# Attention score products in two passes of 128 rows, and where the value and modulation tiles lie

## The chip, the core and the metric

The kernel runs on one NeuronCore of a Trainium2 chip. The metric is device time in microseconds (us) from launch to end, the median of several runs; lower is better. The profile is that of one execution. Its engines are PE (TensorE, matrix products), PEld (the loading of weights into it), DVE (VectorE), ACT (ScalarE), POOL (GpSimd) and SP, whose queue issues most of the loads from memory.

## The reference

Two layers of a diffusion transformer block on 256 latent tokens and 256 context tokens, of width 1024. In each layer one projection feeds four mixers side by side: a Fourier mixer, differential attention, grouped-query attention and a convolution. They are merged by gates, projected once and followed by an MLP with a squared ReLU. The part that matters here is the score products:

```python
def _diff_attention(dq, dk, dv, lam):
    s = jnp.einsum('bqhjd,bkhjd->bhjqk', dq, dk).astype(jnp.float32) * ATTN_SCALE
    p = jax.nn.softmax(s, axis=-1)
    a = (p[:, :, 0] - lam * p[:, :, 1]).astype(dv.dtype)
    return jnp.einsum('bhqk,bkhe->bqhe', a, dv)

def _gqa_attention(gq, gk, gv):
    s = jnp.einsum('bqhgd,bkhd->bhgqk', gq, gk).astype(jnp.float32) * ATTN_SCALE
    p = jax.nn.softmax(s, axis=-1).astype(gv.dtype)
    return jnp.einsum('bhgqk,bkhd->bqhgd', p, gv)
```

The head dimension d is 64. There are 4 differential heads with two score products (j) each, and 8 grouped query heads on 2 key heads. Layer 0 has latent queries on 512 keys and context queries on 256 keys; layer 1 has only the latent queries.

## The kernel before

Everything is fp32, and each product is made of fp32r parts: a number is split into a high part (rounded by ACT, L126 or L129) and a low part (what is left, subtracted by DVE, L127 or L130). An ordinary product (`mm3`, L147) has three passes: high x high (L149), low x high (L150), high x low (L151). Weights come by SP's queue into 3 landing tiles, and are split by ACT and DVE into tiles `wh` and `wl` (`chunk`, L135).

A score product has a contraction of 64, half of the 128 rows. So the kernel stacks the parts: in a stacked tile one half of the rows holds the high part and the other half the low part (`split_stack`, L496). For differential attention `split_twice` (L501) makes three tiles for each q: two with the high part of product j in both halves (L504 and the ACT copy L505), and one with the low parts of both products. `softmax_part` (L531) then runs two passes through `mms` (L154, the matmul is L156): 128 rows, q high against the stacked k, and 64 rows, q low against k high (`diff_front`, L554). For grouped attention (`gqa_front`, L604) the first pass is the stacked q against k high in both halves, and the second has 64 rows, q high against k low.

A planner orders the instructions of each engine ahead of time, by priority and by its own costs, and sets the waits; each engine then runs its own list in order. `attention_part` (L899) makes per layer the convolution projection, the Fourier mixer, the value tiles `dv`, then 4 heads of differential attention (units of 128 queries, the next head's projections and the gates of finished branches filled in between by `fill`), then 4 pairs of grouped heads in the same manner. Taps of the convolution are put on DVE unit by unit.

Tiles of 128x512 are taken from and given back to a pool `rs` (`Slots`, L55; 24 in layer 0, 16 and 14 narrow ones in layer 1). In layer 0 another 4 lie in a region that is lent until differential attention ends (`lent`, L927): the first two of the four pairs of `dv` take these (`rs.lend`), the other two pairs take tiles of `rs`. When the region is given up (L1012), the conditioning rows `srow` are loaded into it (`mods_rows`, L266). They are multiplied on DVE (L287, `mods_dve`) with rows of the modulation weights, which POOL's queue loads (L283) into two landing tiles `wm` (L922) that lie outside the lent region.

Of the kernel before, what the change touches and what calls it, by code (L numbers as in the profile page):

```python
# [9 lines left out]
F = mybir.dt.float32  # L10
R = mybir.dt.float32r
# [8 lines left out]
P = 128  # L20
D = 1024
KT = 8
L = 256
T = 512
# [56 lines left out]
class Body:  # L81
# [20 lines left out]
    def new(self, name, shape, dtype=F, pool=None, space=None):  # L102
        if space is not None:
            pool = getattr(self, "psum", None)
            if pool is None:
                pool = self.psum = self.ec(self.tc.tile_pool(name="psum", bufs=1, space=PSUM))
        return (pool or self.const).tile(shape, dtype, tag=name, name=name)
# [393 lines left out]
    def split_twice(self, dst, src, scale=None):  # L501
        for j in range(2):
            a, b = slice(64 * j, 64 * j + 64), slice(64 - 64 * j, 128 - 64 * j)
            self.split_to(dst[j][a], dst[2][a], src[a], scale)  # L504
            self.nc.scalar.activation(dst[j][b], src[a], AF.Copy, scale=scale or 1.0)  # L505

    def rope_split(self, dst, ps, n, split, gain=None):
        nc = self.nc
        if n > L:
            split([d[:, L:n] for d in dst], ps[:, L:n], gain)  # L510
        raw, sw, t1 = (self.tmp()[:, :L] for _ in range(3))
        if gain is None:
            nc.scalar.copy(raw, ps[:, :L])
        else:
            nc.scalar.activation(raw, ps[:, :L], AF.Copy, scale=gain)  # L515
        nc.vector.stream_shuffle(sw, raw, list(range(16, 32)) + list(range(16)))
        nc.vector.tensor_tensor(t1, raw, self.cos, op=ALU.mult)
        nc.vector.tensor_tensor(sw, sw, self.sin, op=ALU.mult)
        nc.vector.tensor_tensor(t1, t1, sw, op=ALU.add)
        split([d[:, :L] for d in dst], t1)  # L520
# [33 lines left out]
    def diff_front(self, l, s, qt, dq, dk):  # L554
        nc = self.nc
        k0, nk, t0 = self.keys[s]
        er = []
        for j in range(2):
            pr = slice(64 * j, 64 * j + 64)
            q = [x[:, s * L:(s + 1) * L] for x in (dq[j], dq[2][pr])]  # L560
            k = [x[:, k0:k0 + nk] for x in (dk[j], dk[j][pr])]
            er.append(self.softmax_part(q, k, nk, qt))
        (e0, z0), (e1, z1) = er
        r1, c1 = self.sm1(), self.sm1()
        nc.vector.reciprocal(r1, z1)
        nc.vector.scalar_tensor_tensor(c1, z0, self.nlam[:, l:l + 1], r1, ALU.mult, ALU.mult)
        nc.vector.scalar_tensor_tensor(e0, e1, c1, e0, ALU.mult, ALU.add)
        if qt == 0:
            self.zz = self.st4()[:, :2]
        nc.vector.scalar_tensor_tensor(self.zz[:, qt:qt + 1], z0, EPS, z0, ALU.mult, ALU.mult)  # L570
        return e0, self.zz
# [31 lines left out]

    def gqa_front(self, l, j, s, i, qt, gq, gk):  # L604
        k0, nk, t0 = self.keys[s]
        qr = slice(64 * i, 64 * i + 64)
        c = 4 * self.ns * j + 2 * (2 * s + qt) + i
        q = [x[:, s * L:(s + 1) * L] for x in (gq[i], gq[i][qr])]
        k = [x[:, k0:k0 + nk] for x in (gk[j // 2][0], gk[j // 2][1][qr])]
        e, z = self.softmax_part(q, k, nk, qt, self.st32[1][:, c:c + 1])  # L610
        r = self.sm1()
        self.mark = self.nc.vector.reciprocal(r, z).ins.name
        if l or (2 * s + qt) in GACT:
            self.nc.scalar.activation(e, e, AF.Copy, scale=r)
        else:
            self.nc.vector.tensor_scalar(e, e, r, None, ALU.mult)
        return e
# [281 lines left out]
    def attention_part(self, l, n):  # L899
# [11 lines left out]
        with ExitStack() as ctx:  # L911
            pool = ctx.enter_context(tc.tile_pool(name=f"mix{l}", bufs=1, reuse_waits="tile"))
# [5 lines left out]
            spare = new("or", [P, 2 * L])  # L918
            self.oraw = Ring([spare[:, j * L:(j + 1) * L] for j in range(2)])
            self.more_weights(new, 0 if l == 0 else 2)  # L920
            if l == 0:
                wm = self.ring("wmg", NWG, [P, D], pool=pool)  # L922
            lent = ExitStack()
            tiles = [new(f"r{i}", [P, T], R) for i in range(wide)] + [new(f"q{i}", [P, L], R) for i in range(thin)]
            pts = Ring([[new(f"pt{q}{i}", [P, 4, L], R) for q in range(2)] for i in range(2)])
            self.pt = pts
            spool = lent.enter_context(tc.tile_pool(name=f"lent{l}", bufs=1, reuse_waits="tile"))  # L927
            rs = self.rs = Slots(tiles, [self.new(f"e{i}", [P, T], R, spool) for i in range(4 if l == 0 else 0)])
            self.tmps["g"] = self.gring if l == 0 else Ring([g[:, i * L:(i + 1) * L] for g in self.gring.tiles for i in range(2)])

            for k in ((0, 5) if "dbg" in self.a else ()):
# [11 lines left out]
            dv = []  # L943
# [13 lines left out]
            def head(i):  # L957
                def k():
                    dk = self.pair()
                    self.rope_split(dk, self.proj(l, T_DK + i, T), T, self.split_stack)  # L960
                    heads[i] = [dk]

                def q():
                    dq = self.few(n, 3)
                    self.rope_split(dq, self.proj(l, T_DQ + i, n), n, self.split_twice, gain=SCALE)
                    heads[i].append(dq)
                return [k, q]

            gq, box = [], {}
# [38 lines left out]
            self.advance(backs, -1)  # L1008
            if PIPE[0]:
                self.advance(backs)  # L1010
            rs.give(dv[2:] if l == 0 else dv)
            lent.close()  # L1012
            if l == 0:
                spool = ctx.enter_context(tc.tile_pool(name="rows", bufs=1, reuse_waits="tile"))
                self.mods_rows(wm, self.new("srow", [P, 2, D], pool=spool), spare.bitcast(BF))
            gk = box["gk"]
            while backs and not LATE:
# [256 lines left out]
MU, NWG = (6, 1, 0), 2  # L1274
# [117 lines left out]
```

## Time and profile before

| | |
|---|---|
| median of 3 runs | 1547.14 us |
| lowest and highest run | 1542.46 and 1548.66 us |
| span of the profiled execution, first to last instruction | 1540.8 us |
| PE busy | 1486.1 us (96%) |
| DVE busy | 1196.6 us (78%) |
| ACT busy | 793.7 us (52%) |

The profile has no separate time for the profiled execution; its span is set against the median. Matmuls are pipelined: the duration that the profile shows of one is longer than the time from its start to the start of the next, so what PE needs for one is read from the starts. Rows written by one line and one shape family are merged in a timeline (x2 is two instructions), with the shape of the first.

### The profile page before, as it was taken

The page shows a single profiled execution, that of the slowest core. Times are in us where ns is not written, and L with a number is a line of the kernel's source. Part 1 is how long each engine was busy: PE and PEld are TensorE (multiplying, and loading weights), DVE is VectorE, ACT ScalarE, POOL GpSimd, SP SyncE. Part 2 cuts the span into 40 slices and gives each one's busy share as a digit, 9 for nine tenths or more (in the row PEclk, how much of TensorE's full clock was granted, in tenths as well). Part 3 has the DMA queues.
Part 4 walks back from the last instruction along what each step waited for, and adds up shares of the span by engine and source line. Part 5 has one row for each costly group of instructions (what it writes and reads, how often), then busy time and mean ns, then how long its engine had stood idle before and what let it go on. Part 6 is the DMA issues. An engine that isn't in the chain of part 4 may idle for free.

```text
span 1540.8 us, 24989 instructions
## 1 busy us (share of the span) xinstructions
PE 1486.1 (96%) x9242; PEld 1305.5 (85%) x9242; DVE 1196.6 (78%) x2689; ACT 793.7 (52%) x1560; POOL 123.7 (8%) x165
## 2 busy tenths in 40 slices
PE   6999999999999999999999999989999999899997
PEld 4787778777777899898889999988798999899986
DVE  5699887888888958848975577789998976675555
ACT  4335654565554346764432336543665775577643
POOL 0100000002111002201110012100000110000000
PEclk9999999999999999999999999999999999999999
DMA  8522222313334554766775565362232435466552
GB/s 319 179 68 75 66 66 66 110 55 123 100 128 135 191 175 138 238 196 218 241 258 186 190 222 166 105 202 71 86 109 79 138 122 176 134 190 200 165 191 96
DMA packets 74009, 230.01 MB, mean 149 GB/s; under 512 B 8480, under 2 KB 17184, under 8 KB 72608
## 3 DMA queue, kind: packets, MB, share of 16 engines
q1 hardware_dynamic: 60192, 181.10, 36.1%
q0 software_dynamic: 13408, 47.19, 9.4%
q8 instruction: 72, 1.18, 0.3%
q14 instruction: 49, 0.40, 0.1%
q10 hardware_dynamic: 288, 0.14, 0.0%
HBM read 227.35 MB, written 1.05 MB: 148 GB/s over the span
## 4 chain that ended last, share of the span: by engine, by line
PE 86%; DVE 7%; DMA 3%; ACT 2%; issue 1%; SPq 0%; POOL 0%; DVEq 0%; ACTq 0%; POOLq 0%
PE ps_mm L149 22%; PE ps_mm L151 21%; PE ps_mm L150 21%; PE ps_s L156 4%; PE ps_s L438 3%; PE ps_tp L549 2%; PE ps_tp L438 1%; PE ps_o L438 1%; DVE wl L127 1%; PE ps_o L156 1%; PE ps_o L150 1%; PE ps_o L151 1%; PE ps_o L149 1%; PE ps_s L149 1%; PE ps_s L150 1%
## 5 line engine op out<-in xcount | busy, mean ns | idle before, releaser
L126 ACT CAST wh<-raw 128x1024 fp32r<-128x1024 f32 (+3 forms) x283 | 259.7, 919 | 335.1 <-PE ps_mm L150 182.8
L127 DVE TENSOR_TENSOR wl<-raw,wh 128x1024 fp32r<-128x1024 f32 (+3 forms) x283 | 303.6, 1074 | 146.6 <-ACT wh L126 142.4
L149 PE MATMUL ps_mm<-h,wh 128*128 128x512 f32 (+2 forms) x996 | 347.5, 351 | 6.2 <-ACT h L132 4.0
L151 PE MATMUL ps_mm<-h,wl 128*128 128x512 f32 (+2 forms) x996 | 345.8, 347 | 4.0 <-DVE wl L127 3.9
L150 PE MATMUL ps_mm<-h,wh 128*128 128x512 f32 (+2 forms) x996 | 343.9, 345 | 0.0
L149 PEld LDWEIGHTS ps_mm<-h,wh 128*128 128x128 f32 x996 | 190.2, 192 | 34.1 <-issue 4.6
L151 PEld LDWEIGHTS ps_mm<-h,wl 128*128 128x128 f32 x996 | 191.3, 192 | 29.1 <-DVE wl L127 6.5
L150 PEld LDWEIGHTS ps_mm<-h,wh 128*128 128x128 f32 x996 | 191.5, 192 | 21.3 <-DVE h L133 0.6
L127 DVE TENSOR_TENSOR wlx<-raw,whx 128x1024 fp32r<-128x1024 f32 (+2 forms) x85 | 94.0, 1107 | 36.9 <-ACT whx L126 36.8
L126 ACT CAST whx<-raw 128x1024 fp32r<-128x1024 f32 (+2 forms) x85 | 80.9, 953 | 47.7 <-PE ps_mm L150 29.2
L800 DVE SCALAR_TENSOR_TENSOR cy<-cv,half_dw,cy 128x512 f32<-128x512 f32 (+1 forms) x180 | 102.9, 611 | 0.2
L149 PE MATMUL ps_mm<-h,whx 128*128 128x256 f32 (+2 forms) x336 | 99.1, 296 | 3.6 <-ACT tf L515 2.5
L287 DVE SCALAR_TENSOR_TENSOR tl<-wm,srow 128x1024 bf16<-128x1024 f32 x80 | 97.6, 1220 | 0.9
L150 PE MATMUL ps_mm<-h,whx 128*128 128x256 f32 (+2 forms) x336 | 97.6, 291 | 0.0
L151 PE MATMUL ps_mm<-h,wlx 128*128 128x256 f32 (+2 forms) x336 | 97.1, 292 | 0.0
L149 PE MATMUL ps_mm<-r,wh 128*128 128x256 f32 (+1 forms) x260 | 88.1, 339 | 0.1
L151 PE MATMUL ps_mm<-r,wl 128*128 128x256 f32 (+1 forms) x260 | 86.3, 332 | 1.5 <-DVE wl L127 1.5
L150 PE MATMUL ps_mm<-r,wh 128*128 128x256 f32 (+1 forms) x260 | 86.1, 331 | 0.0
L126 ACT CAST hs<-hid 128x256 fp32r<-128x256 f32 x96 | 38.5, 406 | 70.9 <-PE ps_o L438 39.4
L149 PEld LDWEIGHTS ps_mm<-h,whx 128*128 128x128 f32 x336 | 63.5, 189 | 7.5 <-ACT tf L515 2.7
L127 DVE TENSOR_TENSOR hs<-hid,hs 128x256 fp32r<-128x256 f32 x96 | 42.4, 445 | 34.5 <-ACT hs L126 33.9
L856 POOL TENSOR_TENSOR x<-x,tg 128x512 f32<-128x512 f32 (+1 forms) x32 | 37.3, 1165 | 388.4 <-DVE tg L854 309.0
(395 smaller groups left out, 3563.7 us busy)
## 6 DMA issues: line engine op xcount, KB each, us to landing
raw<-in_wff SPq DMA_DIRECT2D x135, 512.0 KB, 4.2
raw<-in_wcol SPq DMA_DIRECT2D x88, 512.0 KB, 3.5
wm<-in_wmodT POOLq DMA_DIRECT2D x56, 512.0 KB, 4.2
wmg<-in_wmodT POOLq DMA_DIRECT2D x24, 512.0 KB, 3.8
raw<-in_wout SPq DMA_DIRECT2D x24, 512.0 KB, 4.1
boot<-in_wmod SPq DMA_DIRECT2D x8, 1024.0 KB, 8.0
raw<-in_wuc SPq DMA_DIRECT2D x16, 384.0 KB, 3.3
raw<-in_wdv SPq DMA_DIRECT2D x8, 512.0 KB, 3.5
```

The lines of the kernel that those rows point to most:

```text
L126: nc.scalar.copy(hi, src)
L127: return nc.vector.tensor_tensor(lo, src, hi.bitcast(F), op=ALU.subtract)
L149: i = nc.tensor.matmul(out, w[0], x[0], start=start, stop=False, skip_group_check=shared)
L150: nc.tensor.matmul(out, w[0], x[1], start=False, stop=False, skip_group_check=shared)
L151: nc.tensor.matmul(out, w[1], x[0], start=False, stop=stop, skip_group_check=shared)
L156: self.nc.tensor.matmul(out[:w.shape[-1]], w, x, start=start and i == 0, stop=stop and i == len(passes) - 1)
L287: i = nc.vector.scalar_tensor_tensor(self.junk, w, 1.0, self.srow[:, s, :], ALU.mult, ALU.mult, accum_out=self.mods[:, l, c, s:s + 1])
L438: self.nc.tensor.matmul(banks[t][i][:, c], x[q][:, tok], w[j][:, a:b], start=start and j + q == 0, stop=stop and q == 1, skip_group_check= ...
L549: nc.tensor.transpose(ps[:, i * P:(i + 1) * P], p[:, i * P:(i + 1) * P], self.ident)
L800: nc.vector.scalar_tensor_tensor(y3, src, w, y3, ALU.mult, ALU.add)
L856: eng.tensor_tensor(mg, mg, th, op=ALU.add)
```

## The change

In `split_twice` the low part of each q gets a tile of its own, and a new ACT instruction copies it into the other half of the rows; a q has four tiles instead of three (`few(n, 4)`). The second pass of a differential score product is the low part of q in both halves against the whole stacked k; it now includes low x low. In `gqa_front` the second pass is the whole stacked q against k low in both halves, again with low x low. So both passes contract over 128 rows.

To make room, the lent region has 8 tiles instead of 4, and holds all four pairs of `dv`; no tile of `dv` is given to `rs` in layer 0 any more. The two landing tiles `wm` are made after the lent region has been given up, in the pool that also holds `srow`.

```diff
@@ split_twice
-            self.split_to(dst[j][a], dst[2][a], src[a], scale)
+            self.split_to(dst[j][a], dst[2 + j][a], src[a], scale)
             self.nc.scalar.activation(dst[j][b], src[a], AF.Copy, scale=scale or 1.0)
+            self.nc.scalar.copy(dst[2 + j][b], dst[2 + j][a].bitcast(F))
@@ diff_front
-            pr = slice(64 * j, 64 * j + 64)
-            q = [x[:, s * L:(s + 1) * L] for x in (dq[j], dq[2][pr])]
-            k = [x[:, k0:k0 + nk] for x in (dk[j], dk[j][pr])]
+            q = [x[:, s * L:(s + 1) * L] for x in (dq[j], dq[2 + j])]
+            k = [dk[j][:, k0:k0 + nk]] * 2
@@ gqa_front
-        qr = slice(64 * i, 64 * i + 64)
-        q = [x[:, s * L:(s + 1) * L] for x in (gq[i], gq[i][qr])]
-        k = [x[:, k0:k0 + nk] for x in (gk[j // 2][0], gk[j // 2][1][qr])]
+        q = [gq[i][:, s * L:(s + 1) * L]] * 2
+        k = [x[:, k0:k0 + nk] for x in gk[j // 2]]
@@ attention_part
-            if l == 0:
-                wm = self.ring("wmg", NWG, [P, D], pool=pool)
...
-            rs = self.rs = Slots(tiles, [self.new(f"e{i}", [P, T], R, spool) for i in range(4 if l == 0 else 0)])
+            rs = self.rs = Slots(tiles, [self.new(f"e{i}", [P, T], R, spool) for i in range(8 if l == 0 else 0)])
...
-                    dq = self.few(n, 3)
+                    dq = self.few(n, 4)
...
-            rs.give(dv[2:] if l == 0 else dv)
+            rs.give([] if l == 0 else dv)
             lent.close()
             if l == 0:
                 spool = ctx.enter_context(tc.tile_pool(name="rows", bufs=1, reuse_waits="tile"))
+                wm = self.ring("wmg", NWG, [P, D], pool=spool)
                 self.mods_rows(wm, self.new("srow", [P, 2, D], pool=spool), spare.bitcast(BF))
```

## Rows read from the trace of the kernel before

**Rows 1.** The page's first part: busy us, share of span, instructions of each engine.
```profile
PE 1486.1 (96%) x9242; PEld 1305.5 (85%) x9242; DVE 1196.6 (78%) x2689; ACT 793.7 (52%) x1560; POOL 123.7 (8%) x165
```

**Rows 2.** The chain of work that ended last, by engine.
```profile
PE 86%; DVE 7%; DMA 3%; ACT 2%; issue 1%; SPq 0%; POOL 0%; DVEq 0%; ACTq 0%; POOLq 0%
```

**Rows 3.** PE's waits: who waited for whom, us in total, times, longest.
```profile
PE ps_mm L151 <- DVE wl L127: 5.5, 7, 1.5
```

**Rows 4.** Windows: stretch, its length, busy us (instructions) by engine, clock, DMA.
```profile
134.00:165.00 31.00, 30.13 (x129) 22.18 (x128) 28.96 (x69) 18.96 (x48) 0.00 (x0) 1.00 0.22 75
165.00:300.00 135.00, 134.91 (x695) 109.34 (x694) 113.47 (x358) 70.93 (x173) 0.53 (x1) 1.00 0.24 74
300.00:480.00 180.00, 178.32 (x849) 140.83 (x848) 150.30 (x354) 99.58 (x197) 27.65 (x26) 1.00 0.32 103
1060.00:1165.00 105.00, 99.54 (x625) 83.83 (x624) 97.91 (x272) 62.35 (x147) 0.00 (x0) 1.00 0.30 99
1165.00:1290.00 125.00, 123.67 (x927) 114.42 (x928) 102.58 (x276) 81.99 (x162) 13.62 (x16) 0.97 0.36 115
```

**Rows 5.** The same windows, PE instructions that write the score tile alone.
```profile
134.00:165.00 31.00, 5.94 (x16) 1.00 0.22 75
165.00:300.00 135.00, 19.48 (x50) 1.00 0.24 74
300.00:480.00 180.00, 24.04 (x62) 1.00 0.32 103
1060.00:1165.00 105.00, 13.85 (x32) 1.00 0.30 99
1165.00:1290.00 125.00, 14.53 (x32) 0.97 0.36 115
```

**Rows 6.** PE's timeline around one score product: start, duration, instruction.
```profile
155.73 0.59 PE L156 MATMUL ps_s<-r,r 128*128 128x256 f32 x2
156.25 0.50 PE L151 MATMUL ps_mm<-r,wl 128*128 128x512 f32 x1
156.59 0.40 PE L149 MATMUL ps_mm<-r,wh 128*128 128x512 f32 x1
156.82 0.40 PE L150 MATMUL ps_mm<-r,wh 128*128 128x512 f32 x1
```

**Rows 7.** The weight loads of the same stretch; in brackets the time without one.
```profile
155.94 0.18 PEld L156 LDWEIGHTS ps_s<-r,r 64*128 64x128 f32 x1 [0.25 <-issue]
156.25 0.19 PEld L151 LDWEIGHTS ps_mm<-r,wl 128*128 128x128 f32 x1
156.36 0.19 PEld L149 LDWEIGHTS ps_mm<-r,wh 128*128 128x128 f32 x1
```

**Rows 8.** Timelines of PE and PEld: value products with 64-column low halves.
```profile
347.34 1.09 PE L156 MATMUL ps_o<-pt,r 128*128 128x256 f32 x8
348.27 0.38 PE L549 MATMUL ps_tp<-consts,ta 128*128 128x128 f32 x2
...
347.92 0.30 PEld L156 LDWEIGHTS ps_o<-pt,r 128*64 128x64 f32 x2
```

**Rows 9.** ACT's copies of high parts (min/median/max ns), and waits, 134 to 300.
```profile
L505 ACT ACTIVATE r<-tf x8: 414/416/418, 144.2 to 233.2; 64x256 fp32r<-64x256 f32 x8
...
ACT r L505 <- DVE r L130: 5.2, 6, 2.3
```

**Rows 10.** PE's timeline at the first scores; in brackets its idle time and releaser.
```profile
144.68 1.36 PE L156 MATMUL ps_s<-r,r 128*128 128x512 f32 x3 [0.87 <-ACT r L505]
```

**Rows 11.** Timelines, landing tile: last value product, first use, landing times, POOL's next.
```profile
293.04 0.28 PE L151 MATMUL ps_o<-pt,r 128*128 128x256 f32 x1
...
L287 DVE SCALAR_TENSOR_TENSOR or<-wmg,srow x48: 1200/1218/2201, 353.0 to 535.6; 128x1024 bf16<-128x1024 f32 x48
DMA to landing us min/median/max: 3.5/3.8/5.8
...
329.40 1.75 POOL L856 TENSOR_TENSOR x<-x,tg 128x512 f32<-128x512 f32 x1 [48.58 <-DVE st L172]
```

## What the change does to the time, told ahead

> **What bounds the kernel now.** I read the busy shares first: TensorE (PE) is busy 1486.1 of 1540.8 us, VectorE (DVE) 1196.6, ScalarE (ACT) 793.7 [rows 1]. The chain that ended last says the same from the other side: 86% of it is PE, 7% DVE, 3% DMA [rows 2]. So PE idles only 54.7 us in all, and the largest wait outside the start-up is small: the third matmul of a weight tile for DVE's low half of that tile, 5.5 us in seven times [rows 3]. A microsecond taken from PE's own work should therefore come off the end, as long as DVE, which makes the low halves, keeps up. Whether it can is read stage by stage [rows 4]: around the score products DVE is busy 28.96 of 31 us, 113.47 of 135, 150.30 of 180, 97.91 of 105 and 102.58 of 125. Those are the five stretches in which score products run [rows 5]: 16 + 50 + 62 + 32 + 32 = 192 matmuls, two passes each, so 96 second passes, and the second pass is the one that contracts over 64 rows (8 + 25 + 31 + 16 + 16).
>
> **What a 64-row pass costs.** In the PE timeline an ordinary matmul of 512 columns starts 0.23 us before the next one (156.59 to 156.82) [rows 6]. A 256-column one takes 0.116: eight start at 347.34 and the next instruction at 348.27 [rows 8]. The score product at 155.73 has two 256-column passes, then a 512-column matmul at 156.25 and another at 156.59 [rows 6]. From 155.73 to 156.59 are 0.86 us; by the ordinary starts it would be 0.116 + 0.116 + 0.23 = 0.46. So **0.40 us** are lost around one 64-row pass. The weight loads show how [rows 7]: the 64-row load at 155.94 came after 0.25 us in which no load was running, the load of the following 128-row matmul at 156.25 started together with that matmul (which then lasted 0.50 instead of 0.40), and only the one at 156.36 runs ahead of its matmul (156.59) again. The prefetch of weights is broken on entering and on leaving the 64 rows.
>
> Is it the rows? Half of the eight matmuls at 347.34 have 64 columns of weights instead of 128 (the low half of the value product; their loads show the shape), and they cost nothing extra [rows 8]. The Trainium skill, "TensorEngine Tiling (Array Packing)", section Key Properties, says that a change of tiling mode drains TensorE, and lists narrower columns among the modes as well as fewer rows. The trace agrees for rows and not for columns; by the page the column-narrow matmuls would have cost something too, but these the change leaves alone, so the sum is the same by both.
>
> **The change part by part.**
>
> *Second passes over 128 rows.* Nothing is added on PE: the same 192 matmuls with the same columns. In the differential heads the low part of q gets a second copy in the other half, so the second pass adds low x low; in the grouped heads the tile that already holds both parts is used whole. Removed: 96 x 0.40 = 38.4 us of PE time, by stretch 3.2, 10.0, 12.4, 6.4 and 6.4. The price was read at 256 columns and is taken for 512 too. I take the gap to be independent of the columns, since what breaks is the load and not the streaming.
>
> *How much of it reaches the end.* DVE's work stays the same, so each stretch can't shrink below DVE's busy time [rows 4]. First stretch: 31 - 3.2 = 27.8 is under DVE's 28.96, so at most 2.0 can come off and I take half, 1.0. Second: 125.0 against 113.47 (91%), I take nine tenths, 9.0. Third: 167.6 against 150.30 (90%), again nine tenths, 11.2. Fourth: 98.6 against 97.91 (99%); it fits on paper only, I take half, 3.2. Fifth: 118.6 against 102.58 (86%), 5.8. Sum **30.2 us**. What is late next in the first and fourth stretch is DVE's low half of a weight tile and its softmax maxima.
>
> *The low copies of q on ACT.* One more ACT instruction per half and column block: in layer 0, 4 heads x 2 blocks x 2 halves = 16, in layer 1, 4 x 1 x 2 = 8. The nearest row is the copy of the high part, 64x256 from SBUF, 0.416 us [rows 9]: 24 x 0.416 = 10.0 us of ACT, which is idle for over a third of the time in every stretch [rows 4]. The wait matters more. Each copy reads what DVE has just written, so ACT, which works in order, stands until DVE has made the low part; behind it stand the high parts of the next weight tiles and the exponentials. The nearest row for such a wait is the high copy on ACT behind a DVE low part: eight of them waited 5.2 us together, 0.65 each, the longest 2.3 [rows 9]. The second pass of the first scores of a layer has no other head's work ahead of it: PE already waited 0.87 us for the last copy of q there [rows 10]. I charge two copies and a wait, 2 x 0.416 + 0.65 = 1.5 us, for the first head of each layer: **3.0 us**. The lower bound is nothing (no instruction is removed, so no gain), the upper one all eight heads: 12 us. The later heads' q is made while PE runs the projections and gates of other work, which is the cover.
>
> *Tiles.* The four low tiles of the last two value tiles now lie in the lent buffers, so the differential heads have four tiles more and use one more each for two heads at a time. By the order of taking and giving back, the tightest moment in layer 0 leaves two tiles where it left none; in layer 1 the narrow tiles run out and the last head's q takes two wide ones. Each tile taken was last read at least a head earlier. Cost: nothing.
>
> *The landing tiles of the modulation weights* now share memory with the value tiles, so their first two loads can't be issued early but only after the last value product of the differential heads: its last matmul starts at 293.04 and takes 0.28 [rows 11]. A load lands within 5.8 us, and the first use is at 353.0 [rows 11]: 53 us of cover. On POOL's queue the two issues move behind the load of the conditioning rows and wait there; behind them stands the first merge addition at 329.40 [rows 11]. It isn't reached. Cost: nothing; without the cover, 5.8 us once.
>
> *Order and clock.* The schedule is made anew, since instructions and dependences differ, so the interleaving of passes will shift somewhat; I can't price that from rows, and I allow 3 us either way. The granted clock is 1.00 in four stretches and 0.97 in the fifth [rows 4], so there is little to gain or lose: back to 1.00 it would be 125 x 0.03 = 3.8 us.
>
> **The sum.** 30.2 - 3.0 = 27.2 us off the profiled execution's span: 1540.8 - 27.2 = 1513.6. The median of the runs is 1547.14, 6.3 above that span (what lies around it, and the spread of 1542.46 to 1548.66). So 1519.9, **1520 us**.
>
> **The rivals.**
>
> *DVE takes half of it.* In in-order engines at nine tenths busy, maxima, low halves and taps come late for one another. For it: the first and fourth stretch, where DVE has no room. Against: in the three others it has 9 to 14%. Half of 27.2: 1547.1 - 13.6 = 1533.5. Chance 0.20.
>
> *The weight load comes onto the path.* If a 128-row load couldn't run ahead of a 128-row matmul that is still working, each second pass would show a load of 0.19 us: 96 x (0.40 - 0.19) = 20.2, and by the same share (27.2 of 38.4) 14.3 us: 1532.8. Rows 7 speak against it: the load at 156.36 runs while the 128-row matmul of 156.25 works. This is what the Trainium skill, "TensorE: Matmul & The Clock Gate", Part 3 (What overlaps and what doesn't), would give, which says that weight loads overlap matmuls in flight only in other row groups; the trace disagrees. Chance 0.02.
>
> *Slower: ACT's waits reach PE.* The point is 30.2 / 24 = 1.26 us lost per copy. A copy and the mean wait are 0.416 + 0.65 = 1.07, just under, if all of it reached PE; with the longest wait it is 0.416 + 2.3 = 2.7, or 65 us in all, the upper bound. At a wait of 1.5 all through: 24 x 1.92 = 46, net 16 slower, 1563. For it: DVE is crowded where q is made. Against: ACT's idle time, and that the waits of the high copies cost PE almost nothing. Chance 0.05.
>
> *The change doesn't do what it says.* If the gaps belong to the score product and not to its rows, the starts stay and the copies come on top: 1547.1 + 3.0 = 1550. Chance 0.04.
>
> *All of it arrives*, with the copies hidden: 1547.1 - 38.4 = 1508.7. Chance 0.09.
>
> **How the numbers follow.** Forecast 0.60 with its own range of 1512 to 1528. The range has to reach over most of the half case and the full case: 1508 to 1536, which holds 0.60 + 0.15 + 0.02 + 0.06 = 0.83. Half a per cent is about what a measurement of this kernel can tell from no change, so faster begins under 1539.4: 0.60 + 0.09 + 0.02 + 0.18 = 0.89. Slower is over 1554.9: 0.05. The rest, 0.06, lies between.
>
> **What would show it.** Right: all score matmuls with 128 rows; the next matmul 0.23 after a 512-column second pass; the busy time of the score matmuls down; the second and third stretch shorter by some 9 and 11 us each; nothing different before 134 us and between 490 and 1060 us. Wrong: starts around the second pass still 0.4 too far apart; PE waits for the new copies of more than 3 us in all; PE waits for low halves well above 5.5 us; POOL's first modulation loads landing after their first use.

## The result, and the profile after

The changed kernel takes 1518.88 us (median of 4 runs, 1514.08 to 1522.11); the kernel before takes 1545.18 in the runs beside it. The ratio is 0.9834 with a 95% interval of 0.9807 to 0.9861, so 25.6 us came off. The span of the profiled execution is 1517.1 us, 23.7 less than before.

The page's busy shares and the chain by engine, after (as [rows 1] and [rows 2] before):

```profile
PE 1454.5 (96%) x9242; PEld 1297.4 (86%) x9242; DVE 1192.3 (79%) x2689; ACT 802.5 (53%) x1584; POOL 123.0 (8%) x165
...
PE 79%; DVE 10%; ACT 4%; DMA 3%; issue 2%; POOL 0%; SPq 0%; DVEq 0%; ACTq 0%; POOLq 0%
```

PE does the same 9242 matmuls in 31.6 us less. But the chain tells that not all of it came through: PE's share of it fell from 86% to 79%, and DVE's and ACT's rose from 7% and 2% to 10% and 4%.

The score products in the instructions that write the score tile (durations in ns as minimum, median and maximum):

```profile
L156 PE MATMUL ps_s<-r,r x148: 278/392/502, 147.3 to 1246.1; 128*128 128x512 f32 x84, 128*128 128x256 f32 x64
...
L156 PE MATMUL ps_s<-r,q x44: 387/398/582, 1067.0 to 1204.8; 128*128 128x512 f32 x44
```

All 192 have 128 rows now. PE's timeline around one of them, with two passes of 256 columns, and the weight loads of the same stretch (as [rows 6] and [rows 7]):

```profile
158.36 0.41 PE L156 MATMUL ps_s<-r,r 128*128 128x256 f32 x2
158.60 0.39 PE L149 MATMUL ps_mm<-h,wh 128*128 128x512 f32 x1
158.83 0.39 PE L150 MATMUL ps_mm<-h,wh 128*128 128x512 f32 x1
...
158.22 0.33 PEld L156 LDWEIGHTS ps_s<-r,r 128*128 128x128 f32 x2
158.48 0.19 PEld L149 LDWEIGHTS ps_mm<-h,wh 128*128 128x128 f32 x1
```

From the first pass to the matmul after the next one are 0.47 us (158.36 to 158.83), where it was 0.86 before [rows 6]: the 0.39 us are gone. The load at 158.48 runs ahead, while the 128-row passes of 158.36 are still at work.

Where the time went, by stages that begin and end with the same instructions in both traces (first score product of a kind of head to the first of the next, or to the last value product):

| stage | before, us | after, us | off | forecast, copies taken off |
|---|---|---|---|---|
| start to first score product | 144.7 | 147.3 | -2.6 | 0 |
| differential heads, layer 0 | 151.7 | 144.1 | 7.6 | 8.5 |
| grouped heads, layer 0 | 194.2 | 187.6 | 6.6 | 11.2 |
| between the layers' heads | 589.1 | 588.0 | 1.1 | 0 |
| differential heads, layer 1 | 96.0 | 91.8 | 4.2 | 1.7 |
| grouped heads, layer 1 | 102.7 | 97.9 | 4.8 | 5.8 |
| rest | 262.4 | 260.3 | 2.1 | 0 |

A second execution of the changed kernel gives 144.1, 187.7, 90.8 and 97.6 us for its four stages of heads.

The four stages after in the windows (columns as in [rows 4]):

```profile
147.30:291.40 144.10, 141.86 (x761) 118.36 (x761) 128.17 (x398) 86.95 (x218) 1.59 (x3) 1.00 0.25 80
291.40:479.00 187.60, 183.53 (x913) 150.31 (x913) 162.97 (x382) 106.05 (x210) 30.44 (x29) 0.99 0.34 109
1067.00:1158.80 91.80, 86.34 (x588) 78.21 (x589) 85.03 (x256) 59.87 (x149) 0.00 (x0) 0.96 0.32 103
1158.80:1256.70 97.90, 96.25 (x766) 92.72 (x766) 85.13 (x233) 72.36 (x143) 12.73 (x15) 1.00 0.39 125
```

So 23.2 us came off in the stages of the score products. How much was freed there can be worked out from PE's starts: from each start to the next, less what the same number of columns takes in an undisturbed row (0.227 us for 512, 0.117 for 256, 0.11 for fewer). Summed over the four stages:

| | before, us | after, us |
|---|---|---|
| all time above the undisturbed starts | 62.4 | 39.2 |
| next to a 64-row pass | 41.6 | 0 |
| other gaps of 0.05 to 0.25 us | 10.1 | 22.3 |
| other gaps over 0.25 us | 12.5 | 18.2 |

What is left between these rows and the first are starts within 0.05 us of the undisturbed ones, in sum -2 and -1 us. Of the new small gaps 4.2 us only moved: a score product behind transposes is recorded as starting early, and its next start late, in both kernels. That leaves 41.6 - 4.2 = 37.4 us freed, 0.39 for each of the 96 passes, and some 14 us that came back as gaps elsewhere. They can be seen in what the weight loads waited for, layer 0, from the first score product to the last value product. Before (the waiter, who it waited for, us in total, times, longest):

```profile
PEld ps_s L156 <- issue: 9.4, 36, 0.4
PEld ps_mm L149 <- issue: 3.4, 14, 0.2
PEld ps_mm L692 <- ACT tf L689: 2.1, 4, 1.0
PEld ps_s L156 <- ACT r L505: 1.5, 2, 1.3
PEld ps_mm L359 <- DVE st L173: 0.9, 1, 0.9
```

And after:

```profile
PEld ps_o L317 <- ACT tf L592: 3.2, 6, 1.4
PEld ps_tp L550 <- DVE pt L127: 2.8, 6, 0.7
PEld ps_s L156 <- ACT r L505: 2.6, 3, 1.3
PEld ps_mm L359 <- DVE st L173: 2.5, 4, 1.4
PEld ps_tp L550 <- issue: 1.5, 1, 1.5
PEld ps_mm L149 <- DVE st L693: 1.4, 1, 1.4
```

"issue" is a wait for nothing that the profile shows; those at the score product and behind it (12.8 us) were the 64-row gaps, and they are gone. In their place stand waits for a named producer: the square of a head's output (L592), the split of the transposed probabilities (L127), the reciprocal root (L173). All waits for named producers sum to 8.6 us before and 18.5 after. A load runs ahead of its matmul, so not all of its wait is lost on PE: PE's own waits in the same stretch sum to 2.6 and 6.6 us. In layer 1 the named waits of the loads don't rise in these two traces, 13.2 us before and 13.4 after.

### The profile page after: what moved, and what is told of

Same layout as the page of the kernel before. It is cut to its first block, busy times and chain, and to the rows that moved or that the text cites. A ratio compares the mean times of both kernels' runs of the same rounds, so it can differ in the third digit from the quotient of the medians.

```text
span 1517.1 us, 25021 instructions
## 1 busy us (share of the span) xinstructions
PE 1454.5 (96%) x9242; PEld 1297.4 (86%) x9242; DVE 1192.3 (79%) x2689; ACT 802.5 (53%) x1584; POOL 123.0 (8%) x165
## 4 chain that ended last, share of the span: by engine, by line
PE 79%; DVE 10%; ACT 4%; DMA 3%; issue 2%; POOL 0%; SPq 0%; DVEq 0%; ACTq 0%; POOLq 0%
PE ps_mm L149 20%; PE ps_mm L150 19%; PE ps_mm L151 19%; PE ps_s L438 3%; DVE wl L127 2%; PE ps_s L156 2%; PE ps_tp L438 1%; PE ps_o L438 1%; PE ps_tp L550 1%; ACT wh L126 1%; PE ps_o L156 1%; PE ps_s L149 1%; PE ps_s L150 1%; PE ps_s L151 1%; PE ps_o L150 1%
## 5 line engine op out<-in xcount | busy, mean ns | idle before, releaser
L127 DVE TENSOR_TENSOR wl<-raw,wh 128x1024 fp32r<-128x1024 f32 (+3 forms) x283 | 304.7, 1078 | 137.5 <-ACT wh L126 135.4
L151 PE MATMUL ps_mm<-h,wl 128*128 128x512 f32 (+2 forms) x996 | 345.1, 347 | 4.7 <-DVE wl L127 4.5
L151 PEld LDWEIGHTS ps_mm<-h,wl 128*128 128x128 f32 x996 | 191.1, 192 | 29.3 <-DVE wl L127 7.9
L127 DVE TENSOR_TENSOR wlx<-raw,whx 128x1024 fp32r<-128x1024 f32 (+2 forms) x85 | 93.9, 1106 | 34.6 <-ACT whx L126 34.4
L799 DVE SCALAR_TENSOR_TENSOR cy<-cv,half_dw,cy 128x512 f32<-128x512 f32 (+1 forms) x180 | 102.7, 610 | 0.2
L287 DVE SCALAR_TENSOR_TENSOR tl<-wm,srow 128x1024 bf16<-128x1024 f32 x80 | 97.6, 1220 | 0.8
L150 PE MATMUL ps_mm<-h,whx 128*128 128x256 f32 (+2 forms) x336 | 97.9, 292 | 0.0
L151 PE MATMUL ps_mm<-h,wlx 128*128 128x256 f32 (+2 forms) x336 | 97.0, 292 | 0.0
L151 PE MATMUL ps_mm<-r,wl 128*128 128x256 f32 (+1 forms) x260 | 86.3, 332 | 1.6 <-DVE wl L127 1.6
L127 DVE TENSOR_TENSOR hs<-hid,hs 128x256 fp32r<-128x256 f32 x96 | 41.8, 439 | 34.5 <-ACT hs L126 33.9
L855 POOL TENSOR_TENSOR x<-x,tg 128x512 f32<-128x512 f32 (+1 forms) x32 | 36.8, 1149 | 354.9 <-DVE tg L853 293.8
```

Of the source, the lines that this page charges most:

```text
L127: return nc.vector.tensor_tensor(lo, src, hi.bitcast(F), op=ALU.subtract)
L150: nc.tensor.matmul(out, w[0], x[1], start=False, stop=False, skip_group_check=shared)
L151: nc.tensor.matmul(out, w[1], x[0], start=False, stop=stop, skip_group_check=shared)
L287: i = nc.vector.scalar_tensor_tensor(self.junk, w, 1.0, self.srow[:, s, :], ALU.mult, ALU.mult, accum_out=self.mods[:, l, c, s:s + 1])
L799: nc.vector.scalar_tensor_tensor(y3, src, w, y3, ALU.mult, ALU.add)
L855: eng.tensor_tensor(mg, mg, th, op=ALU.add)
```

## The experiments

The theory: the 64 rows are the cause; each such pass costs about 0.4 us on PE, and part of what is freed is taken back. Rivals: the moved tiles or the new order bring the gain; the copies on ACT take back; DVE takes back. The ratios below are to the kernel before, run on the same chip in the same series.

**Each half of the score products alone**

```diff
 e1: in the kernel before, gqa_front only
-        qr = slice(64 * i, 64 * i + 64)
         ...
-        q = [x[:, s * L:(s + 1) * L] for x in (gq[i], gq[i][qr])]
-        k = [x[:, k0:k0 + nk] for x in (gk[j // 2][0], gk[j // 2][1][qr])]
+        q = [gq[i][:, s * L:(s + 1) * L]] * 2
+        k = [x[:, k0:k0 + nk] for x in gk[j // 2]]
 e2: the changed kernel with this undone
```

> Only the grouped heads' second pass gets 128 rows: 48 of the 96 passes, no copies, no tile moved. If the rows are the cause and nothing else matters, 48 x 0.40 = 19.2 us of PE time are freed; by the two traces the grouped stages of the changed kernel shrank by 6.6 and 4.8 us, so I expect 11 us off (ratio 0.993). If the gain came from the moved tiles or from the new order of the differential heads: within 3 us of before (0.998 to 1.002).

> The whole change except the grouped heads, whose second pass keeps 64 rows: the other 48 passes, with the copies and the moved tiles. If the rows are the cause, the differential stages' 7.6 and 4.2 us: 12 us off (0.992), and together with the grouped part alone it adds up to the whole change. If what DVE takes back is shared between the parts, the two parts alone bring more than the whole in sum.

Measured: grouped alone 0.9907 (0.9894 to 0.9920), 14.4 us off; differential alone 0.9913 (0.9901 to 0.9926), 13.4 us off. The sum, 27.8, is within the intervals of the whole (25.6). The grouped half has no copies, and no tile is moved for it, so neither is needed for the gain. It brought more alone than I expected: its layer-0 stage took 185.2 us instead of 187.6 in the whole change (194.2 before); 1.6 us of this difference is TensorE's clock (last section). By their stages the grouped half gave 14.9 us and the differential half 12.7, each of the 18.7 that 48 passes free at 0.39. So some 4 us are missing where there are no copies at all, and 6 where there are.

**The tiles alone**

```diff
 the kernel before with
-  ... range(4 if l == 0 else 0) ...
+  ... range(8 if l == 0 else 0) ...
   ...
-  rs.give(dv[2:] if l == 0 else dv)
+  rs.give([] if l == 0 else dv)
 and the ring "wmg" made after lent.close(), in the pool of srow
```

> Only the tiles are moved (value tiles in the lent buffers, modulation landing tiles made later); score products and copies as before. My theory: no difference, within 2 us of before (ratio 0.999 to 1.001), first use of the landing tile unmoved. The rival that the tiles bring part of the gain (freed buffers end waits): 3 us or more off. The rival that the late landing costs: 1 to 6 us slower.

Measured: 1.0000 (0.9987 to 1.0012). The first loads of the landing tile and its first use, in this run:

```profile
L287 DVE SCALAR_TENSOR_TENSOR or<-wmg,srow x48: 1201/1220/2206, 353.4 to 536.3; 128x1024 bf16<-128x1024 f32 x48
...
L283 POOL DMA_DIRECT2D wmg<-in_wmodT x24: 530/570/576, 293.8 to 529.2; - x24
```

The load is issued at 293.8, behind the last value product, and the first use is at 353.4 where it was 353.0 before [rows 11]. The tiles cost nothing and bring nothing; they make room.

**The rows alone**

```diff
 the changed kernel with
-            q = [x[:, s * L:(s + 1) * L] for x in (dq[j], dq[2 + j])]
-            k = [dk[j][:, k0:k0 + nk]] * 2
+            pr = slice(64 * j, 64 * j + 64)
+            q = [x[:, s * L:(s + 1) * L] for x in (dq[j], dq[2 + j][pr])]
+            k = [x[:, k0:k0 + nk] for x in (dk[j], dk[j][pr])]
 and gqa_front as before
```

> The changed kernel with the second passes back at 64 rows, but copies, four tiles for q and moved tiles kept (the copies are made and not read). If the rows are the cause, the whole gain is gone and the copies' cost is left: ratio 1.000 to 1.002 to before, starts around the second pass 0.40 us longer again. If the gain came with the tiles or the order: stays near 0.983.

Measured: 1.0003 (0.9989 to 1.0018). The whole gain goes with the rows. The waits of the weight loads in layer 0, in the same stage as above, have the old first lines again:

```profile
PEld ps_s L156 <- issue: 8.9, 35, 0.4
PEld ps_mm L149 <- issue: 3.4, 14, 0.2
```

This is the experiment that settles the cause: same tiles, same copies, same number of matmuls and columns; only the rows of the second pass differ. It also shows that 24 copies that nobody waits for cost nothing that can be told from the spread of the runs.

Set against the changed kernel, this run shows as well how a part comes back, since PE's sequence in the stages of layer 0 is the same in 99% of the entries. One chain goes from the last matmul of a head's output (L151) over its square on ACT (L593 here, L592 in the changed kernel) to the load of the square as weights (L317). With 64 rows, then with 128:

```profile
262.40 0.28 PE L151 MATMUL ps_o<-pt,e 128*128 128x256 f32 x1
263.45 0.50 ACT L593 ACTIVATE tf<-ps_o 128x256 f32<-128x256 f32 x1
264.45 0.64 PEld L317 LDWEIGHTS ps_o<-consts,tf 128*128 128x128 f32 x4
...
255.93 0.28 PE L151 MATMUL ps_o<-pt,e 128*128 128x256 f32 x1
256.99 0.50 ACT L592 ACTIVATE tf<-ps_o 128x256 f32<-128x256 f32 x1
257.54 0.52 PEld L317 LDWEIGHTS ps_o<-consts,tf 128*128 128x128 f32 x4 [0.39 <-ACT tf L592]
```

Between the two PE has the same ten matmuls, of which two were the 64-row passes. The square ends 1.56 us after the start of L151 in both. With 64 rows PE comes to it only later, and nothing waits; with 128 rows PE is there first, and the load waits 0.39 us. For the seven squares in this stage the time from product to square is the same within 0.3 us; PE starts right behind the square (0.05 us) in two of the seven with 64 rows and in five with 128. The named waits of the loads in layer 0 are 9.6 us in this run against 18.5.

**Does DVE take back the rest?** Both kernels with half of the convolution's taps:

```diff
-            taps = [(j, k) for k in range(TAPS) for j in range(3)]
+            taps = [(j, k) for k in range(0, TAPS, 2) for j in range(3)]
-TAPD, TAPG, PER = (6, 8), (6, 12), ...
+TAPD, TAPG, PER = (3, 4), (3, 6), ...
```

> The kernel before with every second tap of the convolution left out (16 of 31 per channel block, half the pace), so DVE has some 52 us less to do, nearly all of it in the stages of the score products. It is the base for the next run. PE bounds those stages, so little should come off: 2 to 8 us (0.995 to 0.999).

> The changed kernel with the same taps left out. Theory that DVE's crowding takes back what PE frees: with DVE lighter the change brings more, 33 to 38 us against the run before it (e6) instead of 26. Rival that the freed PE time is smaller than 0.40 a pass, or is lost to something DVE has no part in (order, clock, ACT): the difference stays at 24 to 28 us.

Measured: before with half the taps 1539.77 (0.9984, 0.9972 to 0.9996), after with half the taps 1517.92 (0.9843, 0.9824 to 0.9861). The difference is 21.9 us, not the 33 to 38 of the theory, and somewhat under the rival's 24 to 28 too. The test is weaker than I meant it. DVE is busy 41 and 38 us less in the two whole programs, but only 20 and 19 less in the four stages, and not at all in the grouped heads of layer 0 (163.6 us with and without the edit in the kernel before). So it speaks against DVE's load in the other stages alone; the next pair lightens that stage as well. The waits for named producers in layer 0 rise here too, from 9.9 to 20.9 us.

**Are the softmax chains too long?** Both kernels without the row maximum:

```diff
+        self.zero = new("zero", [P, 1])
+        nc.vector.memset(self.zero, 0.0)
         ...
-        nc.vector.tensor_reduce(nm, ps, AX.X, ALU.max, negate=True)
-        if scale is not None:
-            m, nm = nm, self.sm1()
-            nc.vector.tensor_scalar(nm, m, scale, None, ALU.mult)
+        nm = self.zero
         ...
-        nc.scalar.activation(e, ps, AF.Exp, bias=nm, scale=1.0 if scale is None else scale, accum_out=z)
+        nc.scalar.activation(e, ps, AF.Exp, bias=nm, scale=1e-3, accum_out=z)
```

> The changed kernel itself, to stand beside the next three on one chip: 0.983 to before (0.981 to 0.986).

> The kernel before without the row maximum of the scores: the exponential takes a constant bias and a small constant scale, so the chain from score product over softmax to transpose lacks a DVE reduction of 0.4 to 0.7 us and its hand-over. Base for the next run. In the kernel before, the gaps around the 64-row passes cover the chains (its weight loads waited little for named producers), so little comes off: 0 to 5 us.

> The changed kernel without the row maximum. Theory that chains of fixed length, over which PE's order has the same number of instructions as before but now less time, take back the missing PE time: shorter chains let more of it through, so the difference to the run before it (e10) is 29 to 36 us. Rival that what is lost is not in the softmax chains (norm chains, clock, order): 23 to 28 us, as without the edit.

Measured: the changed kernel again 1516.55 (0.9827, 0.9811 to 0.9842), 26.8 off; before without the maximum 1531.69 (0.9927, 0.9909 to 0.9944); after without it 1507.67 (0.9782, 0.9761 to 0.9804). The difference of the last two is 24.0 us (22.4 by the ratios), about the rival's 23 to 28 and not the 29 to 36 of the theory. Shorter chains help both kernels (by 12 and 9 us) and let no more of the change through. The 12 us are a miss too: I expected 0 to 5, since the 64-row gaps were to cover the chains. The edit also takes 49 and 47 us off DVE's busy time in the four stages, 17 and 15 of them in the grouped heads of layer 0, so which of the two brings the 12 us is not separated, and this pair is at the same time the wider test of DVE's load: **DVE's load in sum is not what takes back**, and this part of my reasoning fell. In the differential heads of layer 1 alone DVE stayed at nine tenths (82.5 of 90.2 us), so for that stage it is not tested. The waits of the weight loads after, without the maximum:

```profile
PEld ps_o L319 <- ACT tf L591: 4.2, 7, 1.4
PEld ps_tp L549 <- DVE pt L127: 3.2, 6, 1.1
PEld ps_s L156 <- ACT r L507: 2.7, 3, 1.3
PEld ps_mm L361 <- DVE st L173: 2.5, 3, 1.6
```

They are the same producers with about the same times (line numbers shift by one or two). In sum, layer 0: 8.1 us before and 18.2 after. So in three pairs, each planned anew with other loads and other chains, the waits for named producers rise by about 10 us when the 64 rows go (8.6 to 18.5, 9.9 to 20.9, 8.1 to 18.2). In layer 1 they rise less evenly: 13.2 to 13.4, 9.5 to 15.4, 9.2 to 12.9.

**The copies twice, and two tries at the waits**

```diff
 e4: the line  self.nc.scalar.copy(dst[2 + j][b], dst[2 + j][a].bitcast(F))  stands twice
 e8: GACT = (0, 1)  ->  GACT = (0, 1, 2, 3)
 e12: split of pt, square of po and rstd_of of diff_back  under  self.tc.high_priority(2 * WPRIO)
```

> The changed kernel with each low copy of q made twice on ACT: 24 more instructions of 0.41 us, 10 us of ACT, in the same places and behind the same waits. If the copies are hidden: within 2 us of the changed kernel (0.983 to 0.985 to before). If the copies are on the path, as I charged for the first heads: 2 to 3 us slower. If ACT takes back the missing 12 us: 5 to 10 us slower.

> The changed kernel with the scaling of the grouped probabilities of the context queries in layer 0 on ACT instead of DVE: 16 multiplications of 128x256, 0.35 us each, so 5.6 us less on DVE and about as much more on ACT. If DVE's crowding in the grouped stage of layer 0 takes back PE time, this brings 1 to 4 us (0.981 to 0.983 to before). If not: no difference.

> The changed kernel with three links of the chains ahead of other work in the planner's order: the split of the transposed probabilities, the square of a differential head's output, and its reciprocal root. By the theory of the chains the waits for them (PE and its loads for the split, the square and the root) shrink from some 8 us and 2 to 5 us come off (0.980 to 0.982 to before). If the chains wait for their inputs and not in a queue: no difference. If the priority pushes weight tiles back: slower.

Measured: copies twice 0.9892 (0.9875 to 0.9909); scaling on ACT 0.9869 (0.9852 to 0.9887); chains first 0.9893 (0.9876 to 0.9911); the changed kernel 0.9834 and 0.9827 (the latter in the series of the chains, the former in one of its own). None is faster. A second copy of each low part costs some 9 us by the ratios, whose intervals lie at least 2 us apart; by the stages of the profiled executions it is 2.2 us in the differential heads of layer 0 and 3.4 in those of layer 1. So on this path 24 more ACT instructions of 0.4 us are not hidden; that the first copy isn't altogether either is likely, but not shown. This is what I had put down for ACT taking back the missing 12 us. It can't be the whole of it, since the grouped half without copies missed 4 us too. The direct trace of the first copy in the changed kernel is small: the loads of scores waited 0.9 us for it. The scaling on ACT left its own stage as it was (188.6 us for 187.6). The priority shortened the grouped heads of layer 0 (184.8 us for 187.7) and lengthened the differential heads of both layers, by 3.5 us in layer 0 and by 7 in layer 1 (97.8 for 90.8). There PE waits for other links, of which these are the largest:

```profile
PE ps_o L317 <- ACT or L594: 2.1, 1, 2.1
PE ps_tp L550 <- DVE ta L568: 1.5, 1, 1.5
PE ps_o L150 <- DVE pt L127: 1.2, 1, 1.2
```

## Why the prediction was right, point by point

*The cause and its price: right.* 0.40 us per pass was forecast from one score product; over all passes it is 0.39, and 37.4 us in sum for the 38.4. That 256 and 512 columns cost the same held too (0.49 at the median for both, counted with the 0.08 us by which many starts are shifted). Undoing the rows alone takes the whole gain back.

*Rows and not columns: right.* The value products' matmuls with 64 columns of weights are still there, 80 of them, and cost nothing: value products that follow one another start 0.117 us apart at the median, whichever their columns. The Trainium skill, "TensorEngine Tiling (Array Packing)", Key Properties, would have both drain, if 64 columns are the mode 128x64 of its list of configurations; for columns the trace says no.

*How much reaches the end: the number right, the reason wrong.* I let 30.2 of 38.4 through, and took DVE's busy time as the floor. The four stages gave 23.2 with the copies, where I had 27.2. That the time came out within about 1 us of the forecast is luck in part: what lacks there is made up by the stages without score products and by the spread of the runs (below). In the grouped stage of layer 0, where I put DVE's room at 10%, only 6.6 us came for 11.2 (the clock takes 1.6 us of it, see the last section); in the differential stage of layer 1, where DVE had no room on paper, 4.2 came for 1.7. Lightening DVE let no more through. What stands in its place by the traces: PE runs its list, which the planner wrote with nearly the same order (95% of the entries of layer 0's stages stand in the same sequence), faster between a product and the point where its result is needed; what ACT and DVE make in between takes as long as before; so waits for named producers appear that the 64-row gaps had covered. For the squares this is shown by the pair of traces above. That the planner puts each consumer at about the time at which it holds the result to be ready, without counting the gaps, would explain why shorter chains and a lighter DVE don't help, since it then puts the consumers earlier too. This last step is argued and was not tried. About 4 of the 14 us are not assigned by the named waits; by the stages they lie in layer 1, where 3.5 of 12.5 freed us are missing and these waits don't rise, and their cause stays open.

*The copies: charged 3.0 us.* Named waits for them are 0.9 us, the second copy of each costs 5.6 us by the profiled stages and some 9 by the ratios. The 3.0 is neither shown nor refuted: the half with copies missed 2 us more than the half without, and how much of that the copies make stays open, since the form without them needs other instructions in its place.

*Tiles and modulation loads: right.* 1.0000 alone. After the change the two first loads are issued at 288.60 and first used at 348.5, a cover of 60 us.

*What I allowed for and what came.* The first score product came 2.6 us later in this execution, in the start-up, in which nothing is changed: its first modulation load landed 1.1 us later, and behind it PE ran for 3.4 us, from 27.8, at 1.2 GHz where it had 2.4 before. Between the heads 1.1 and in the rest 2.1 us came off that I had not forecast; in the second execution of the changed kernel the rest took 261.8, so most of the 2.1 is spread between executions. Together with the four stages that makes 23.7 by the spans, and the runs differ by 25.6 (by the ratio) to 26.8. The spans give less since the profiled execution before was the fastest of its runs: a run takes 1.7 to 1.8 us more than its span wherever both are recorded, so the 1540.8 belong by all signs to the 1542.46. Of the 6.3 us that the forecast adds to the span, 4.6 are thus spread.

*The rivals.* Half of it (13.6), nothing, or slower: excluded by the ratio. All of it: no. The weight load on the path: excluded by the load at 158.48.

## What to carry to other kernels

Look at what starts late around a matmul that uses fewer rows than its neighbours: the price is on both sides of it and was the same for 256 and 512 columns here, so it is worth filling the rows, even with a term that the sum doesn't need, when the pass is short and stands between full ones. When PE's own gaps are removed in a list that stays in order, expect a part back as waits for the chains that the gaps had covered; here some 14 of 37 us came back, of which about 10 show as such waits. And test the explanation of a shortfall as well as that of the gain, and look in the trace whether the test reached the stage it was meant for: a busy engine beside the bound one looked like the reason and, where it was made lighter, wasn't.

## What the runs showed of the hardware

A 64-row pass between 128-row matmuls costs PE 0.39 us at 2.4 GHz (mean of 96). A pass whose weights have 64 columns and 128 rows costs none. Once in the kernel before, two 64-row passes on different halves of the rows stood next to each other: they started 4 ns apart, at 1097.39, and the next matmul of 128 rows at 1097.82, so the pair took about the time of one and lost the 0.4 us once.

In the changed kernel the granted clock was at 1.2 GHz for 3.4 us in the first grouped heads, where it was at 2.4 in the kernel before. In the windows:

```profile
296.90:300.40 3.50, 2.58 (x16) 1.93 (x14) 3.17 (x12) 1.68 (x3) 0.00 (x0) 1.00 0.02 7
300.80:304.20 3.40, 3.40 (x10) 2.63 (x9) 3.26 (x11) 2.33 (x6) 0.00 (x0) 0.51 0.26 74
```

And PE's timeline there:

```profile
297.73 0.95 PE L691 MATMUL ps_mm<-consts,tf 128*128 128x2 f32 x8
298.54 0.95 PE L156 MATMUL ps_s<-r,r 128*128 128x512 f32 x3
300.43 0.50 PE L149 MATMUL ps_mm<-h,wh 128*128 128x512 f32 x1 [0.95 <-DVE st L693]
...
301.97 0.63 PE L150 MATMUL ps_mm<-h,wh 128*128 128x512 f32 x1
302.40 0.63 PE L151 MATMUL ps_mm<-h,wl 128*128 128x512 f32 x1
```

Ahead of it PE ran eight matmuls of two columns, which sum the squares of the queries, then three passes of scores, and then waited 0.95 us until DVE had read the sums (L693). Matmuls then start 0.43 us apart instead of 0.23; eight of them make 1.6 us. It came in the same place in the second execution of the changed kernel and not in the grouped half alone, where that stage was 2.4 us shorter. It is not the freed rows that bring it: it came there too in the two runs whose grouped heads keep 64 rows but have the tiles and the copies of the change (the differential half at 300.2 us, the rows alone at 309.0), behind a wait of 0.48 us at the same instruction. So it goes with the new order of this place, and against the rows alone the stage is shorter by 8.4 us (196.0 to 187.6), not by 6.6.
